# A hybrid sequence layer: convolution gates copied out by ScalarE, output projection summed in PSUM, second half of the merge and early P stages in written order

## The chip, the cores and the metric

One core of a Trainium2 chip runs the whole kernel. The metric is device time in microseconds, the median of the runs; a profiled execution is a run of its own. TensorE multiplies into PSUM (8 banks, each one output tile of 128x512 float32); VectorE and ScalarE read PSUM; GpSimd works on SBUF alone; transfers are queued on SyncE and ScalarE. Each engine takes its instructions strictly in its queue's order.

## The reference, cut to what matters

```python
h = rmsnorm(x, g_pre_mix)                     # x: 1024 tokens x 1024
proj = h @ w_in                               # u | conv x, B, C | q, k, v, forget | gates (3 x 1024)
ya = s5_mixer(u, ...)                         # 32 groups, 64 states each, scan over tokens
yb = B * conv3_causal(C * x_conv)             # 512 channels
yc = forgetting_attention(q, k, v, forget)    # 8 heads
merged = sum_b sigmoid(gate_b) * (y_b @ w_branch[b])
x = x + rmsnorm(merged @ w_out, g_post_mix)
x = x + rmsnorm(relu(rmsnorm(x, g_pre_mlp) @ w_ff1)**2 @ w_ff2, g_post_mlp)
```

All is float32. A product runs as three float32r products of high and low halves (high x high, high x low, low x high), so every weight tile is split: ScalarE writes the high half (H), VectorE or GpSimd subtracts to get the low half (L).

## The kernel before, in words

- **Head.** Tokens come in 8 tiles of 128 (t0 to t7). For each, ScalarE squares and sums (`x_square`), eight small operations make the inverse square root (`rsqrt1`, L79), and `x_norm` (L338) writes a diagonal matrix dg of it; `x_tr` (L361) multiplies a tile by its dg, which transposes and scales it at once. `x_split` makes hT, high and low.
- **Projections.** `proj_stream` (L263) hands out weight tiles of 128 columns, each times both halves of the tokens (th = 0, 1), 24 products per half, into two PSUM banks (tag `pj`). The consumer empties the bank: `conv_cons` (L798) for the convolution's x, c and b (four steps j), `gate_cons` for the 24 gates g. In between, generators for the S5 branch are run by a clock that the program keeps itself (`spawn`, `poll`): a generator yields the time after which it is to go on. For c and b VectorE multiplies from the bank: vp = p_cc x xs, later ac = p_cb x ac.
- **V.** At L888 the two weight blocks wv1 and wv0 are split, with 16 projection steps between them, and `v_group` multiplies them. Gates stay on ScalarE.
- **Attention**, then the **merge**: for each half th, pair dp of column tiles and branch b, `merge_item` (L1217) multiplies y_b by wb, gates it (gl, ma) and adds on GpSimd; the last branch splits the sum into m, high and low.
- **Output projection.** `rows_item` (L1258) multiplies m by w_out, four tiles of contraction (kc) and half the columns (e) at a time: for kc 0 ScalarE copies the bank to acc, for kc 1 VectorE adds the bank to acc. In the second half `wo_last` does kc 1 for both e (weights wol, and woeh/woel split ahead from woer).
- **mix(t)** (L1282), per token tile: square of acc, inverse square root on GpSimd (n_t), scale by it and gpost (VectorE), add x (xr; GpSimd for t0 to t3, VectorE for t4 to t7), a second square and root, hr = acc x root x gmlp, then eight transposes (pth) and the operands of the first feed-forward product: h2 for t0 to t3, and for t4 to t7 the combinations tb, tm and T1 to T4, high and low. These are a Strassen-like scheme with seven products: P1 needs only h2, P6 and the others need T of all four late tokens. The mixes of t0 to t3 run under the second half of the merge, those of t4 to t7 under wol and the P1/P2 stages (`Pair.run_a`, weights wa0 to wa7).
- **Order.** Outside of blocks under `manual_schedule`, a scheduler may move instructions within each engine's queue; inside, the order of the program holds. In the program before, only the head and V stand in such blocks.

```python
tt(vp[:, 2 + th * HALF:2 + (th + 1) * HALF], ps, cvt["xs"][:, sl], MUL)    # L811
if accumulate: tt(dst, ps, dst, ADD)                                        # rows_item
tt(acc, acc, xr_, ADD, dve if th else pool)                                 # mix
yield MY1 if th else 8.0
```

## Time and profile before

| | |
|---|---|
| median of three runs | 1694.05 us (1692.35, 1694.05, 1694.09) |
| profiled execution | 1695.55 us, its span 1693.8 |
| TensorE busy | 1622.6 us (96%), 7815 instructions |
| VectorE busy | 1032.2 us (61%), 1548 |
| ScalarE busy | 693.6 us (41%), 1042 |
| GpSimd busy | 501.9 us (30%), 603 |

The span is the time from the first to the last instruction in the trace. Busy shares are means over stages with different limits; which wait ends last in a stage is read from the trace of that stage. The granted clock is the share of full speed that TensorE was given: 1.00 is 2.4 GHz, 0.50 is 1.2 GHz, values between are means over a stretch.

### The profile page before, as it was taken

The page shows a single profiled execution, that of the slowest core. Times are in us where ns is not written, and L with a number is a line of the kernel's source. Part 1 is how long each engine was busy: PE and PEld are TensorE (multiplying, and loading weights), DVE is VectorE, ACT ScalarE, POOL GpSimd, SP SyncE. Part 2 cuts the span into 40 slices and gives each one's busy share as a digit, 9 for nine tenths or more (in the row PEclk, how much of TensorE's full clock was granted, in tenths as well). Part 3 has the DMA queues.
Part 4 walks back from the last instruction along what each step waited for, and adds up shares of the span by engine and source line. Part 5 has one row for each costly group of instructions (what it writes and reads, how often), then busy time and mean ns, then how long its engine had stood idle before and what let it go on. Part 6 is the DMA issues. An engine that isn't in the chain of part 4 may idle for free.

```text
span 1693.8 us, 21052 instructions
## 1 busy us (share of the span) xinstructions
PE 1622.6 (96%) x7815; PEld 1334.8 (79%) x7815; DVE 1032.2 (61%) x1548; ACT 693.6 (41%) x1042; POOL 501.9 (30%) x603
## 2 busy tenths in 40 slices
...
GB/s 162 122 42 77 83 68 103 108 99 7 216 174 142 213 47 218 117 168 58 255 262 97 193 205 91 138 163 189 183 181 143 166 344 373 254 199 195 178 100 50
DMA packets 186034, 261.73 MB, mean 155 GB/s; under 512 B 24752, under 2 KB 108764, under 8 KB 183884
## 3 DMA queue, kind: packets, MB, share of 16 engines
...
q8 instruction: 61, 1.00, 0.2%
q14 instruction: 41, 0.34, 0.1%
...
## 4 chain that ended last, share of the span: by engine, by line
PE 64%; DVE 9%; POOL 5%; DMA 5%; issue 4%; ACT 3%; SPq 1%; DVEq 0%; ACTq 0%; POOLq 0%
PE p_g L122 13%; PE P L122 11%; PE pb L122 3%; PE p_q L122 3%; PE pv L122 3%; PE P4f L122 3%; PE P7f L122 3%; PE P3f L122 3%; PE P6f L122 3%; PE P5f L122 3%; PE P2f L122 3%; PE P1f L122 2%; PE ps L122 2%; PE av L122 2%; PE pt L126 2%
## 5 line engine op out<-in xcount | busy, mean ns | idle before, releaser
L65 DVE TENSOR_TENSOR st<-x,st 128x1024 fp32r<-128x1024 f32 x70 | 86.7, 1250 | 77.4 <-ACT st L73 74.4
L122 PE MATMUL p_g<-hT,w_g_1H 128*128 128x512 f32 x384 | 126.4, 407 | 5.1 <-ACT g L831 3.5
L122 PE MATMUL p_g<-hT,w_g_0H 128*128 128x512 f32 x384 | 126.9, 406 | 2.8 <-DVE ac L65 2.8
L73 ACT ACTIVATE st<-x 128x1024 fp32r<-128x1024 f32 x70 | 73.6, 1059 | 98.5 <-PE P6f L122 16.6
L65 POOL TENSOR_TENSOR w2s<-w2s 128x512 f32<-128x512 f32 x32 | 44.0, 1375 | 232.1 <-DMA w2s<-in_w_ff 232.1
L65 POOL TENSOR_TENSOR s<-w1r 128x512 f32<-128x512 f32 x32 | 52.4, 1659 | 167.4 <-DMA w1r<-in_w_ff 156.4
L122 PE MATMUL pb<-yH,wb_0L 128*128 128x512 f32 x192 | 77.5, 403 | 11.8 <-DVE wb_0L L65 11.7
L65 DVE TENSOR_TENSOR sl<-x,sh 128x1024 fp32r<-128x1024 f32 x42 | 56.6, 1352 | 47.4 <-ACT sh L73 47.4
L122 PEld LDWEIGHTS p_g<-hT,w_g_1H 128*128 128x128 f32 x384 | 69.3, 192 | 17.5 <-ACT g L831 4.0
L122 PEld LDWEIGHTS p_g<-hT,w_g_0H 128*128 128x128 f32 x384 | 70.0, 191 | 14.8 <-DVE ac L65 3.2
L122 PE MATMUL pb<-yH,wb_0H 128*128 128x512 f32 x192 | 77.0, 401 | 2.1 <-DVE macc L68 2.1
L65 POOL TENSOR_TENSOR fa<-fa,gfin 128x512 f32<-128x512 f32 x16 | 25.5, 1606 | 178.0 <-ACT fjk L1654 178.0
L122 PE MATMUL p_g<-hT,w_g_1L 128*128 128x512 f32 x192 | 76.6, 399 | 0.0
L122 PE MATMUL pb<-yL,wb_0H 128*128 128x512 f32 x192 | 76.6, 399 | 0.0
L122 PE MATMUL p_g<-hT,w_g_0L 128*128 128x512 f32 x192 | 76.5, 398 | 0.0
L65 DVE TENSOR_TENSOR PT<-pt,PT 128x512 fp32r<-128x512 f32 (+2 forms) x96 | 53.0, 552 | 26.7 <-ACT PT L73 26.1
L73 ACT ACTIVATE PT<-pt 128x512 fp32r<-128x512 f32 (+2 forms) x96 | 47.0, 490 | 47.9 <-PE pt L126 43.5
L73 ACT ACTIVATE sh<-x 128x1024 fp32r<-128x1024 f32 x42 | 44.2, 1058 | 51.4 <-PE P3f L122 9.9
L1023 ACT ACTIVATE P<-ps,mx 128x128 f32<-128x128 f32 (+3 forms) x64 | 47.4, 740 | 32.0 <-DVE mx L1020 31.9
L65 POOL TENSOR_TENSOR macc<-macc,gl 128x512 f32<-128x512 f32 x16 | 27.8, 1748 | 101.6 <-DVE gl L68 101.6
L1020 DVE TENSOR_REDUCE mx<-ps 128x1 f32<-128x128 f32 (+3 forms) x64 | 48.1, 752 | 13.2 <-PE ps L122 13.1
L122 PEld LDWEIGHTS pb<-yH,wb_0L 128*128 128x128 f32 x192 | 37.0, 193 | 21.7 <-DVE wb_0L L65 13.9
(831 smaller groups left out, 4631.6 us busy)
## 6 DMA issues: line engine op xcount, KB each, us to landing
...
```

The costliest lines, as they stand in the source:

```text
L65: (eng or dve).tensor_tensor(o, x, y, op=op)
L73: act.activation(hi, src, AF.Copy, scale=scale)
L122: pe.matmul(o, l, r, start=start, stop=stop)
L126: pe.transpose(o, i, idn)
L1020: dve.tensor_reduce(mx, sv, axis=mybir.AxisListType.XY, op=MAX, negate=True)
L1023: act.activation(Pm[:, 0:kend].rearrange("p (c n) -> p c n", c=nch), sv, AF.Exp, bias=mx, accum_out=sm)
```

## The change

- Head: t1's root on GpSimd, the low half of w_u0 on VectorE; t4 to t7 are scaled in place (two on ScalarE, two on VectorE) and transposed with the identity.
- Convolution: ScalarE copies p_cc and p_cb to SBUF (vp, bs); VectorE multiplies 128x1024 from SBUF; xs has three buffers, vp and ac two.
- V: 12 projection steps ahead of the wv1 split, 20 (was 16) between the splits.
- Output projection: both halves of the contraction go to one bank, which stays open (`wps`); ScalarE copies it to acc after the second.
- From the output projection of the first half to the end of the early P stages VectorE, ScalarE, GpSimd and TensorE run in written order. The split of the last branch is spawned 2.0 later; mix has more yields; late mixes are spawned 4.0 apart (`MS`); P1 and P2 tiles are written one by one with the weight preparation of later pairs between them (`ff1_early`); one tile operation fewer makes tm. hr of all late tokens shares two buffers.

```diff
-    def x_norm(t0, n):
+    def x_rs(t0, n, eng=None):
...
+    def x_diag(t):
...
-        mm(o, xt[t][:, kt * P:(kt + 1) * P], dgs[t], True, True, 0.22)
+        if t < 4:
+            mm(o, xt[t][:, kt * P:(kt + 1) * P], dgs[t], True, True, 0.22)
+        else:
+            transp(o, xt[t][:, kt * P:(kt + 1) * P], ident)
...
-            x_norm(t, 1)
+            x_rs(t, 1, pool if t == 1 else None)
...
-                tt(vp[:, 2 + th * HALF:2 + (th + 1) * HALF], ps, cvt["xs"][:, sl], MUL)
+                act.activation(vp[:, 2 + th * HALF:2 + (th + 1) * HALF], ps, AF.Copy)
                 if th == 1:
-                    ac = cvt["ac"] = cv.tile([P, L], F, name=f"ac{j}", tag="ac")
+                    tt(vp[:, 2:], vp[:, 2:], cvt["xs"], MUL)
+                    ac = cvt["ac"] = cv.tile([P, L], F, name=f"ac{j}", tag="ac", bufs=2)
...
-                ac = cvt["ac"]
-                tt(ac[:, sl], ps, ac[:, sl], MUL)
+                act.activation(cvt["bs"][:, sl], ps, AF.Copy)
                 if th == 1:
+                    ac = cvt["ac"]
+                    tt(ac, ac, cvt["bs"], MUL)
...
+        for _ in range(12):
+            next(ps_)
         split(wv[1][1], wv[1][2], wv[1][0])
-        for _ in range(16):
+        for _ in range(20):
...
+    def merged(hi, lo, m):
+        split(hi, lo, m, scale=0.5)
+        yield 0.0
...
-                    split(mT[0, th, dt_ // 4][:, dt_ % 4, :], mT[1, th, dt_ // 4][:, dt_ % 4, :], macc[d], scale=0.5)
+                    spawn(merged(mT[0, th, dt_ // 4][:, dt_ % 4, :], mT[1, th, dt_ // 4][:, dt_ % 4, :], macc[d]), 2.0)
...
-                ps = mps(f"{name}p{t}")
+                if k0 == 0:
+                    wps[t, e] = mps(f"{name}p{t}")
+                ps = wps[t, e]
...
-                if accumulate:
-                    tt(dst, ps, dst, ADD)
-                else:
-                    act.activation(dst, ps, AF.Copy)
+                if k0:
+                    act.activation(accs[t][:, e * HALF:(e + 1) * HALF], ps, AF.Copy)
...
+        yield 1.5
         hr = hrow[0](f"hr{t}")
         rs = rms_scale(acc, hr, f"n1_{t}")
+        yield 5.0
         stt(acc, acc, rs, mixg[0], MUL, MUL)
         tt(acc, acc, xr_, ADD, dve if th else pool)
-        yield MY1 if th else 8.0
+        yield 2.5 if th else 5.0
         rs2 = rms_scale(acc, hr, f"n2_{t}")
         act.dma_start(x1_s[t], acc)
+        yield 5.0
         stt(hr, acc, rs2, mixg[1], MUL, MUL)
...
-        yield MY2 if th else 12.0
+        yield 5.0
...
-            tt(tm[:, 1], b12, tk["D"][:, :, cs], ADD)
...
-            stt(tm[:, 1], b22, -1.0, tm[:, 1], MUL, ADD)
+            tt(tm[:, 1], tk["D"][:, :, cs], tb[:, 0], SUB)
...
-                        spawn(mix(t))
+                        spawn(mix(t), MS * (t % 4))
...
+    def ff1_early(p, nxt):
+        p[0].run_p1()
+        nxt[0]()
+        yield
+        p[0].run_p2()
+        yield
+        p[1].run_p1()
+        nxt[1]()
+        yield
+        p[1].run_p2()
+        yield
...
+    ordered = tc.manual_schedule(engines={mybir.EngineType.DVE, mybir.EngineType.Activation, mybir.EngineType.Pool, mybir.EngineType.PE})
+    ordered.__enter__()
     new_acc(range(4), lt)
...
+    for i in range(0, KC, 2):
+        nxt = [p.prep_a for p in pairs[i + 2:i + 4]] if i + 2 < KC else [s_[0] for s_ in stages[:AH]]
+        for _ in ff1_early(pairs[i:i + 2], nxt):
+            poll()
+    settle()
+    ordered.__exit__(None, None, None)
```

How the queues move at three places. In the rows a number behind an underscore is the program's buffer number; of a name such as acc_8737 the number tells tokens apart.

VectorE's queue at the first convolution step, before (vp, ac and w_cc as above; CA belongs to the S5 branch):

```order
L65 TENSOR_TENSOR CA_1128<-CA_1128,Cx_1129 128x1152
L758 MEMSET S_1416 128x8
L65 TENSOR_TENSOR vp_1167<-p_cc_00_1107,xs_1076 128x512
L65 TENSOR_TENSOR vp_1167<-p_cc_01_1170,xs_1076 128x512
L60 TENSOR_SCALAR ac_1196<-vp_1167,cwcol 128x1024
L65 TENSOR_TENSOR w_cc_0L<-r_cc_1200,w_cc_0H 128x1024
L68 SCALAR_TENSOR_TENSOR ac_1196<-vp_1167,cwcol,ac_1196 128x1024 x2
L65 TENSOR_TENSOR ac_1196<-p_cb_00_1202,ac_1196 128x512
```

and now:

```order
L65 TENSOR_TENSOR CA_1124<-CA_1124,Cx_1125 128x1152
L771 MEMSET S_1415 128x8
L65 TENSOR_TENSOR w_cc_0L<-r_cc_1197,w_cc_0H 128x1024
L65 TENSOR_TENSOR vp_1163<-vp_1163,xs_1072 128x1024
L60 TENSOR_SCALAR ac_1193<-vp_1163,cwcol 128x1024
L68 SCALAR_TENSOR_TENSOR ac_1193<-vp_1163,cwcol,ac_1193 128x1024 x2
L65 TENSOR_TENSOR Kq_1253<-Kq_1253,dg 16x8x16
L65 TENSOR_TENSOR w_cb_0L<-r_cb_1336,w_cb_0H 128x1024
L65 TENSOR_TENSOR ac_1193<-ac_1193,bs_1228 128x1024
```

The products from PSUM are gone from the queue; two products of 128x1024 from SBUF have come, and the three operations of ac stand together.

ScalarE's queue at the start of V, before (g: gates; wvH: the high half of wv1, then of wv0; so: S5's output):

```order
L785 ACTIVATE so_3038<-pz_3029 128x1024
L73 ACTIVATE wvH_3078<-r_wv_2660 128x2112
L831 ACTIVATE g_3092<-p_g_00_3022,bgcol 128x512
L832 DMA gt_s_115<-g_3092 128x512
L831 ACTIVATE g_3120<-p_g_01_3095,bgcol 128x512
L832 DMA gt_s_115<-g_3120 128x512
L73 ACTIVATE w_g_0H<-r_g_3020 128x1024
L73 ACTIVATE wvH_3082<-r_wv_3080 128x2048
```

and now:

```order
L798 ACTIVATE so_3046<-pz_3037 128x1024
L848 ACTIVATE g_3098<-p_g_00_3030,bgcol 128x512
L849 DMA gt_s_115<-g_3098 128x512
L848 ACTIVATE g_3126<-p_g_01_3101,bgcol 128x512
L849 DMA gt_s_115<-g_3126 128x512
L73 ACTIVATE wvH_3086<-r_wv_2668 128x2112
L73 ACTIVATE w_g_0H<-r_g_3028 128x1024
```

Both halves of a gate tile now stand ahead of the first wvH.

VectorE's queue in the late mixes, before (acc_8741 to acc_8744 are tokens 4 to 7, hr_8916, hr_8968 and the two hr_9027 their rows):

```order
L68 SCALAR_TENSOR_TENSOR hr_8916<-acc_8741,n_4r,gmlp 128x1024
L65 TENSOR_TENSOR acc_8744<-wl_9042,acc_8744 128x512
L68 SCALAR_TENSOR_TENSOR acc_8743<-acc_8743,n_6r,gpost 128x1024
L65 TENSOR_TENSOR acc_8744<-wl_9056,acc_8744 128x512
L65 TENSOR_TENSOR acc_8743<-acc_8743,xr_9025 128x1024
L68 SCALAR_TENSOR_TENSOR hr_8968<-acc_8742,n_5r,gmlp 128x1024
L68 SCALAR_TENSOR_TENSOR acc_8744<-acc_8744,n_7r,gpost 128x1024
L65 TENSOR_TENSOR wa1L<-w1h_8945,wa1H 128x1024
L65 TENSOR_TENSOR acc_8744<-acc_8744,xr_9084 128x1024
L65 TENSOR_TENSOR o_0_9139<-P_0_9126,s_0_9111 128x512
L68 SCALAR_TENSOR_TENSOR hr_9027<-acc_8743,n_6r,gmlp 128x1024
L68 SCALAR_TENSOR_TENSOR hr_9027<-acc_8744,n_7r,gmlp 128x1024
```

and now, from the row of token 5 on (acc_8736 to acc_8738 are tokens 5 to 7):

```order
L68 SCALAR_TENSOR_TENSOR hr_9002<-acc_8736,n_5r,gmlp 128x1024
L65 TENSOR_TENSOR wa4L<-w1h_9192,wa4H 128x1024
L68 SCALAR_TENSOR_TENSOR acc_8737<-acc_8737,n_6r,gpost 128x1024
L65 TENSOR_TENSOR acc_8737<-acc_8737,xr_9075 128x1024
L65 TENSOR_TENSOR o_2_9216<-P_2_9203,s_2_9177 128x512
L65 TENSOR_TENSOR tb_9245<-pth_9234,b11f 128x512
L65 TENSOR_TENSOR tm_9244<-pth_9239,tb_9245 128x512
L65 TENSOR_TENSOR tb_9245<-pth_9239,tb_9245 128x512
L65 TENSOR_TENSOR tm_9244<-bdf,tb_9245 128x512
L65 TENSOR_TENSOR B_9092<-pth_9239,B_9091 128x4x128
L65 TENSOR_TENSOR T_9088<-tm_9244,T_9087 128x4x128
L65 TENSOR_TENSOR T_9090<-tb_9245,T_9089 128x4x128
```

The four rows hr stood close together, ahead of wa2L; now each token's work and the low half of a later weight alternate. hr of token 6 follows seven rows further on, behind the last two T, wa5L, o_3 and the scale and add of token 7.

## Rows read from the trace of the kernel before

**Rows 1.** The timeline of TensorE, two starts: the first product of each of two groups of four output tiles (48 products of 128x512 lie between them). Columns, in this and every timeline below: start in us, duration in us, engine, line, operation, output<-inputs, shape, count, and in brackets the engine's idle time before it and who ended it.

```profile
1004.73 0.39 PE L122 MATMUL wo100p<-wo_0H,m 128*128 128x512 f32 x1
...
1015.61 0.39 PE L122 MATMUL wo101p<-wo_0H,m 128*128 128x512 f32 x1
```

**Rows 2.** Busy time by stretches of 20 us: width, busy us (and instructions) of TensorE, its weight loads, VectorE, ScalarE and GpSimd, then the granted TensorE clock, DMA share and GB/s.

```profile
100.00:120.00 20.00, 17.39 (x70) 13.88 (x69) 11.25 (x12) 1.06 (x1) 19.53 (x32) 0.91 0.19 53
...
920.00:940.00 20.00, 17.87 (x76) 14.28 (x75) 11.51 (x11) 5.55 (x9) 11.45 (x25) 0.91 0.48 157
...
960.00:980.00 20.00, 11.29 (x52) 8.82 (x51) 14.30 (x13) 5.69 (x10) 12.41 (x18) 0.88 0.44 143
...
980.00:1000.00 20.00, 20.00 (x82) 16.29 (x82) 13.34 (x18) 7.34 (x11) 9.06 (x11) 0.86 0.78 270
...
1060.00:1080.00 20.00, 12.45 (x52) 9.94 (x53) 12.51 (x14) 7.89 (x14) 11.52 (x24) 0.73 0.34 96
...
1080.00:1100.00 20.00, 20.00 (x98) 16.69 (x98) 18.20 (x29) 15.09 (x25) 0.00 (x0) 1.00 0.54 161
```

**Rows 3.** The timeline of TensorE at its waits from the head to the start of the attention's V.

```profile
15.82 1.16 PE L122 MATMUL ptx<-dg,x 128*128 128x128 f32 x8 [0.81 <-ACT dg L345]
...
110.35 0.73 PE L122 MATMUL p_cb<-hT,w_cb_0H 128*128 128x512 f32 x2 [2.61 <-DVE vp L65]
...
149.88 0.73 PE L122 MATMUL p_cb<-hT,w_cb_0H 128*128 128x512 f32 x2 [1.09 <-DVE vp L65]
...
206.62 0.73 PE L122 MATMUL p_cx<-hT,w_cx_0H 128*128 128x512 f32 x2 [2.72 <-DVE ac L65]
...
250.27 0.72 PE L122 MATMUL p_g<-hT,w_g_0H 128*128 128x512 f32 x2 [2.80 <-DVE ac L65]
...
373.17 0.73 PE L122 MATMUL p_g<-hT,w_g_1H 128*128 128x512 f32 x2 [3.54 <-ACT g L831]
```

**Rows 4.** VectorE and ScalarE at the first convolution step.

```profile
109.62 0.67 DVE L65 TENSOR_TENSOR vp<-p_cc,xs 128x512 f32<-128x512 f32 x1
...
107.55 1.06 ACT L73 ACTIVATE w_cc_0H<-r_cc 128x1024 fp32r<-128x1024 f32 x1 [7.62 <-PE p_cc L122]
```

**Rows 5.** ScalarE at the start of V.

```profile
370.57 1.96 ACT L73 ACTIVATE wvH<-r_wv 128x2112 fp32r<-128x2112 f32 x1 [9.42 <-DMA ya_s<-so]
...
372.44 0.67 ACT L831 ACTIVATE g<-p_g,bgcol 128x512 f32<-128x512 f32 x1
```

**Rows 6.** TensorE at its waits in the second half of the merge.

```profile
926.70 0.50 PE L122 MATMUL pb<-yH,wb_0L 128*128 128x512 f32 x1 [2.13 <-DVE wb_0L L65]
...
958.51 0.50 PE L122 MATMUL pb<-yH,wb_0L 128*128 128x512 f32 x1 [0.85 <-DVE wb_0L L65]
...
965.76 0.50 PE L122 MATMUL pb<-yH,wb_0L 128*128 128x512 f32 x1 [1.48 <-DVE wb_0L L65]
...
979.62 0.80 PE L122 MATMUL pb<-yH,wb_0L 128*128 128x512 f32 x1 [7.23 <-DVE wb_0L L65]
```

**Rows 7.** VectorE, and in the last row GpSimd, in the second half of the merge.

```profile
955.40 3.05 DVE L65 TENSOR_TENSOR wb_0L<-r_wb,wb_0H 128x1024 fp32r<-128x1024 f32 x1
...
973.42 2.27 DVE L68 SCALAR_TENSOR_TENSOR acc<-acc,n_3r,gpost 128x1024 f32<-128x1024 f32 x1 [2.73 <-POOL n_3r L62]
...
976.21 3.35 DVE L65 TENSOR_TENSOR wb_0L<-r_wb,wb_0H 128x1024 fp32r<-128x1024 f32 x1
...
984.59 1.22 DVE L65 TENSOR_TENSOR wb_0L<-r_wb,wb_0H 128x1024 fp32r<-128x1024 f32 x1
...
975.77 2.72 POOL L65 TENSOR_TENSOR acc<-acc,xr 128x1024 f32<-128x1024 f32 x1 [1.16 <-DVE acc L68]
```

**Rows 8.** TensorE at its waits in the P stages.

```profile
1066.25 0.79 PE L122 MATMUL P<-h,wa1L 128*128 128x512 f32 x1 [11.95 <-DVE wa1L L65]
...
1070.68 1.11 PE L126 MATMUL pth<-ident,hr 128*128 128x128 f32 x8
...
1076.30 0.50 PE L122 MATMUL P<-h,wa2L 128*128 128x512 f32 x1 [1.30 <-DVE wa2L L65]
...
1111.70 0.50 PE L122 MATMUL P<-h,wa7L 128*128 128x512 f32 x1 [0.40 <-DVE wa7L L65]
```

**Rows 9.** VectorE in the late mixes and the P stages.

```profile
1050.19 1.28 DVE L68 SCALAR_TENSOR_TENSOR hr<-acc,n_4r,gmlp 128x1024 f32<-128x1024 f32 x1 [2.00 <-POOL n_4r L62]
...
1100.64 0.68 DVE L65 TENSOR_TENSOR o<-P,s 128x512 f32<-128x512 f32 x1
...
1102.37 0.68 DVE L65 TENSOR_TENSOR tb<-pth,b11f 128x512 f32<-128x512 f32 x1
```

**Rows 10.** ScalarE there.

```profile
1096.61 1.06 ACT L73 ACTIVATE wa6H<-w1h 128x1024 fp32r<-128x1024 f32 x1 [1.24 <-DMA w1h<-in_w_ff]
...
1100.57 0.58 ACT L1329 ACTIVATE tb<-pth 128x512 f32<-128x512 f32 x1
...
1101.36 0.63 ACT L1416 ACTIVATE o<-o 128x512 f32<-128x512 f32 x1 [0.21 <-DVE o L65]
...
1041.83 1.04 ACT L1176 ACTIVATE hr<-acc 128x1024 f32<-128x1024 f32 x1
```

**Rows 11.** GpSimd there: the first and the last of the eight small operations of one inverse square root.

```profile
1034.10 0.19 POOL L62 TENSOR_SCALAR n_4q<-n_4q 128x1 f32<-128x1 f32 x1 [22.29 <-ACT hr L1176]
...
1036.80 0.29 POOL L62 TENSOR_SCALAR n_4r<-n_4t,n_4r 128x1 f32<-128x1 f32 x1
```

More of the change, by code (lines that the diff above doesn't have):

```diff
@@ L336, in x_square @@
         act.activation(jk, xt[t], AF.Square, accum_out=xsq[:, t:t + 1])
-    def x_norm(t0, n):
+    def x_rs(t0, n, eng=None):
         sl = slice(t0, t0 + n)
-        rsqrt1(xrs[:, sl], xsq[:, sl], xtm[:, sl])
-        for t in range(t0, t0 + n):
-            dgs[t] = xp.tile([P, P], F, name=f"dg{t}", tag="dg", bufs=8)
-            if t == 3:
-                act.activation(dgs[t], ident, AF.Copy, scale=xrs[:, t:t + 1])
-            else:
-                ts(dgs[t], ident, xrs[:, t:t + 1], MUL)
+        rsqrt1(xrs[:, sl], xsq[:, sl], xtm[:, sl], eng)
+    def x_diag(t):
+        dgs[t] = xp.tile([P, P], F, name=f"dg{t}", tag="dg", bufs=4)
+        if t == 3:
+            act.activation(dgs[t], ident, AF.Copy, scale=xrs[:, t:t + 1])
+        else:
+            ts(dgs[t], ident, xrs[:, t:t + 1], MUL)
     pxs = {}
@@ L374, in hybrid_layer @@
             x_square(t)
-            if t == 3:
-                ut_tiles[0].split(pool)
-            x_norm(t, 1)
+            x_rs(t, 1, pool if t == 1 else None)
             if t == 0:
+                x_diag(0)
                 dve.tensor_copy(gcol, pgc[:, 0:KT])
+            elif t == 2:
+                x_diag(1)
+                x_diag(2)
+        ut_tiles[0].split()
+        x_diag(3)
         ut_tiles[1].split(pool)
@@ L389, in hybrid_layer @@
             x_square(t)
-        x_norm(4, 4)
+        x_rs(4, 4)
+        for t in range(4, NT):
+            if t % 2:
+                ts(xt[t], xt[t], xrs[:, t:t + 1], MUL)
+            else:
+                act.activation(xt[t], xt[t], AF.Copy, scale=xrs[:, t:t + 1])
     def x_rest():
@@ L803, in f @@
                 if th == 0:
-                    cvt["xs"] = cv.tile([P, L], F, name=f"xs{j}", tag="xs")
+                    cvt["xs"] = cv.tile([P, L], F, name=f"xs{j}", tag="xs", bufs=3)
                 act.activation(cvt["xs"][:, sl], ps, AF.Copy)
@@ L1353, in wo_item @@
         last = kc == 1 and e == 1
-        return rows_item(f"wo{th}{kc}{e}", wo_k, 4 * kc, e, range(4 * th, 4 * th + 4), lhs, kc == 1,
+        return rows_item(f"wo{th}{kc}{e}", wo_k, 4 * kc, e, range(4 * th, 4 * th + 4), lhs,
                          (lambda t: spawn(mix(t), 10.0 * (t % 4))) if last else None)
@@ L1370, in run @@
                         xh, xl = lhs(t, k)
-                        mm(ps, xh, wh, k == 0, False, 0.214)
+                        mm(ps, xh, wh, False, False, 0.214)
                         mm(ps, xh, wl, False, False, 0.214)
                         mm(ps, xl, wh, False, k == 3, 0.214)
-                    dst = accs[t][:, e * HALF:(e + 1) * HALF]
-                    tt(dst, ps, dst, ADD)
+                    act.activation(accs[t][:, e * HALF:(e + 1) * HALF], ps, AF.Copy)
                     if e:
-                        spawn(mix(t))
+                        spawn(mix(t), MS * (t % 4))
                     if (t, e) == WP:
-                        stages[0][0]()
+                        pairs[0].prep_a()
                     yield
@@ L1478, in run_a, with run_p1, run_p2 @@
             yield
+        def run_p1(self):
+            i = self.i
+            if i % 2 == 0:
+                s1t[i // 2] = lt.tile([P, 2, HALF], F, name=f"s1_{i}", tag=f"acc{(i // 2) % 4}")
+            self.s1 = s1t[i // 2][:, i % 2]
+            self.p1 = prod(f"P1_{i}", self.wa, 0, h2[0, 0], h2[1, 0])
+            act.activation(self.s1, self.p1, AF.Copy)
+        def run_p2(self):
+            i = self.i
+            p2 = prod(f"P2_{i}", self.wa, 4, h2[0, 1], h2[1, 1])
+            o = lt.tile([P, HALF], F, name=f"o11_{i}", tag="row", bufs=3)
+            tt(o, p2, self.s1, ADD)
+            put_a(i, "P1", o)
+            self.a11 = None
         def run_b1(self):
@@ L1522, in run_b3, with ff1_stages @@
             yield
-    def ff1_stages():
-        ps_ = [Pair(i) for i in range(NF)]
+    def ff1_early(p, nxt):
[9 more added lines that the diff above has]
+        yield
+    def ff1_stages(ps_):
         A = lambda p: [(p.prep_a, p.run_a)]
@@ L1528, in ff1_stages @@
         st = []
-        for p in ps_[:KC]:
-            st += A(p)
         for p in ps_[:KC]:
@@ L1740, in hybrid_layer @@
     r2 = r2_es.enter_context(pool_("r2"))
-    hlate = []
-    def hr_tile(name):
-        t = int(name[2:])
-        if t < 6:
-            return r2.tile([P, D], F, name=name, tag="hr", bufs=2)
-        if not hlate:
-            hlate.append(ws.tile([P, 2, D], F, name="hr67", tag="raw", bufs=2))
-        return hlate[0][:, t - 6, :]
-    hrow[0] = hr_tile
-    stages = ff1_stages()
+    hrow[0] = lambda name: r2.tile([P, D], F, name=name, tag="hr", bufs=2)
+    pairs = [Pair(i) for i in range(NF)]
+    stages = ff1_stages(pairs)
     run_items(wo1[:1], wo1[1:])
```

23 lines of the change are left out of this document (11 added, 12 removed).

## The prediction, as put on record before the changed kernel ran

> **What bounds the kernel now.** I read the busy shares first, then the busy time by stretches with TensorE's granted clock, then TensorE's waits one by one, and at each wait the queue of the engine named. TensorE is busy 96% of the span, so only its waits, and the stretches at half clock behind them, can be won. At full clock 48 products of 128x512 take 1015.61 - 1004.73 = 10.88 us, 2.72 for an output tile of 12 [rows 1], and eight transposes 1.04 [rows 8]. In 1080:1100 the clock is 1.00. In 100:120, which has one wait of 2.61, it is 0.91 on average: part of the stretch ran at 1.2 GHz instead of 2.4, and 0.09 x 20 = 1.8 us went with it [rows 2, 3]. I charge these 1.8 to each wait over 2 us and nothing to shorter ones.
>
> The losses that the change aims at:
> - **Convolution:** waits of 2.61, 1.09, 2.72 and 2.80, all on VectorE's vp or ac [rows 3]: 9.2, with three half-clock stretches of 1.8 14.6.
> - **Start of V:** 3.54 on a ScalarE gate [rows 3], with 1.8 behind it 5.3.
> - **Merge, second half:** 2.13, 0.85, 1.48 and 7.23, all on VectorE's wb_0L [rows 6]: 11.7; the clock of 920:940 (0.91) adds 1.8, that of 980:1000 (0.86 of a stretch without a wait) 2.8 [rows 2]: 16.3.
> - **Late mixes and P stages:** wol starts at 1015.61 + 10.9 = 1026.5. From there eight wol tiles, sixteen P tiles and four sets of transposes are 24 x 2.72 + 4 x 1.04 = 69.5 us of work, to 1096.0. The trace resumes after its last wait here at 1111.70 [rows 8] with 20 products of the last pair open and 8 of P6_0 and its followers issued early: 12 net, 2.7 us, so 1114.4. Lost: 18.4, of which 11.95 in one wait for wa1L.
>
> Together 54.6 us.
>
> **Part by part.** *Head.* Token 1's inverse square root goes to GpSimd: eight small operations in 3.0 us [rows 11], beside VectorE's for token 2 instead of ahead of it, so dg3, which ends the 0.81 wait [rows 3], is free earlier. The diagonals of tokens 1 and 2 come later, and their products fill that gap. Between nothing and 0.8 I take 0.3. Tokens 4 to 7 are scaled whole, two on ScalarE and two on VectorE (two instructions of about 1.06 each [rows 10]); their transposes replace as many products: nothing, hidden behind ut projections; 1 us if that cover is short.
>
> *Convolution.* TensorE waits because a PSUM bank of the projection is emptied by VectorE, which stands in its queue behind S5 work (vp starts at 109.62, right behind a CA). In the new order ScalarE copies these banks; it is busy 1.06 us of 100:120 [rows 2, 4], so a copy (about 0.6, like o and tb [rows 10]) starts when the tile ends. VectorE exchanges four PSUM operations of 0.67 a step [rows 4] for two of 128x1024 (1.22 [rows 7]), no more work. All four waits go. Late next is the S5 state for py: its VectorE chain was covered by projection tiles together with the waits that vanish. I keep back 0.6 for it: **14.0** (11 to 14.6).
>
> Here a rule speaks against the edit. Row first: the same 128x1024 subtraction takes 1.22 us at 984.59, and 3.05 and 3.35 at 955.40 and 976.21; the last runs beside a GpSimd addition (975.77, 2.72) [rows 7]. GpSimd is busy 19.53 of 100:120 [rows 2]. The Trainium skill, page "GPSIMD Engine Reference", section "Key points", says that GpSimd shares its SBUF interfaces with VectorE and contends with VectorE instructions that have two SBUF inputs. The new products vp x xs and ac x bs are of that kind, while the old ones took one input from PSUM; the trace agrees with the rule in the three rows named. By 1.22 each they cost nothing that TensorE sees; by 3.05 to 3.35 the eight of them add some 15 to 17 us to VectorE's queue, a part of which the S5 chain hands on. I stay near the first, since nothing but S5 waits for them, and the second sets the lower end of 11.
>
> *Start of V.* Twelve steps of the gate projection now stand before the wv1 split. In the old queue the split (370.57, 1.96 us) waits for the ya_s transfer, and gate g starts at 372.44 behind it [rows 5]; in the new one two gates pass first. The wait of 3.54 and its 1.8 go; the wv split in front of the following gate may cost 0.5. **4.8** (3.5 to 5.3). The 48 products that move ahead of the attention are the same work; later gate numbers shift through the attention, +-1.5, which I count as nothing.
>
> *Output projection in PSUM.* Sixteen VectorE additions of about 0.68 [rows 9] become ScalarE copies of 0.6. TensorE never waited for them; their worth is room on VectorE in the next part. All eight banks are held to the second half; those copies follow at once.
>
> *Merge in written order.* VectorE's queue no longer puts a token's scale, which waits for GpSimd (2.73 idle before 973.42), ahead of the next weight's low half at 976.21 [rows 7]. I followed the written queues pair by pair. With E the end of the output projection, six tiles are 16.3 and the transposes of token 0 end at E+17.4. ScalarE then copies h2 twice and b11f (0.6 each), the last behind a VectorE subtraction of 0.68, and splits wb111 (1.06): E+20.5; VectorE's low half 1.22: E+21.7. TensorE has two tiles first and wants it with the third product of pb121, at 17.4 + 5.4 + 0.5 = E+23.3. The slack of 1.6 is the smallest that I found. A contended low half (3.05 for 1.22) eats it, so I leave 2.5 us of waits over: **13.8** (8 to 16.3).
>
> *wol.* woeh and woel now stand ahead of wol on both queues and wait for the woer transfer: 0.5 lost (0 to 1.5).
>
> *Late mixes.* The queues are written, so a token's row hr can only come after all that stands before it. I walk them from the start of wol, A, with 1.28 for a scale, 1.22 for an add or low half, 0.68 for a PSUM tile on VectorE, 1.06 for a high half, 1.1 for a square, 0.6 for a tile on ScalarE, 3.0 for an inverse square root [rows 7, 9, 10, 11].
> - hr5: ScalarE's square of token 4 stands behind a copy of acc5 and wa0H (A+10.9), its second square behind a copy of acc6 (A+18.0); hr4 is at 22.3. wa1H follows the last wol copy, wa2H the copy of P1_0 (26.2); wa2L 27.4, token 5's scale and add 29.9, o11_0 30.6, on ScalarE its two operations and tb4 32.4, VectorE's four tile operations 35.1, T4 and the second square of token 5 36.8, s1 and wa3H 38.5, wa3L, o11_1, hr5: 41.7. TensorE wants hr5 at 21.8 + 6 x 2.72 + 1.04 = 39.2: a wait of 2.5.
> - hr6: from hr5 on s1_2 (whose buffer was acc5's), wa4H, wa4L, scale and add of token 6, o11_2, its two ScalarE operations, a square of token 7, tb5, four tile operations, T4, the square of token 6, s1, wa5H, wa5L, o11_3, scale and add of token 7, hr6: 20.7 us in one chain. TensorE has 1.04 + 4 x 2.72 = 11.9: a wait of 8.8.
> - hr7: the same way 12.8 us against 1.04 + 3 x 2.72 = 9.2: a wait of 3.6. The half-clock stretch behind it costs 1.8; those behind the first two vanish in the next wait.
>
> New losses 2.5 + 8.8 + 3.6 + 1.8 + 0.5 = 17.2 against 18.4: **1.2** (-6 to 18). One tile operation a token less is in the walk. The wait for wa1L goes; what is late next is hr6.
>
> **Sum:** 0.3 + 14.0 + 4.8 + 13.8 + 1.2 = 34.1. The profiled execution took 1695.55, so 1661.4; it lies 1.5 above the median of the runs shown (1694.05): **1660**.
>
> **Rivals.**
> 1. *The P stages flow.* If the row chains overlap better than my walk (a ScalarE queue that is free when I hold it blocked), all of the 18.4 goes: 51.3 saved, median 1642.8. For it: the old stage from 1080 on runs without a wait at VectorE 18.20 of 20 [rows 2], so the throughput is there. Against: the new order spreads the same latency chains over the tiles that want their ends. 0.2.
> 2. *Contention.* Low halves at 3.05 where GpSimd works: merge 8, convolution 11, V 4, late stage 0 with 0.3: 23.3 saved, 1670.7; with the late stage 5 worse 1676. This is the mechanism of the rule above. For it: 19.53 of 20 in 100:120 and the two slow rows. 0.2.
> 3. *Slower: the written ScalarE queue stalls the merge.* A token's second square waits for GpSimd's addition, and the next pair's high half stands behind it. If a token's GpSimd work (two inverse square roots of 3.0, one addition of 2.72 and four of the merge) passes the 17.4 us of a pair, the lag grows and each of four pairs waits like the 7.23 with its 2.8: 40 instead of 16.3; rows 3 us later each add some 10 to the late stage. Net 23.7 + 10 - 19.1 = 14.6 lost: 1708.6. Against it: GpSimd is busy 9 to 12.4 of 20 there [rows 2], about 10 of 17.4. 0.04.
> 4. *It does not do what it says:* ScalarE, kept in order, reaches the copies late, and the convolution waits stay half: 7 lost from the sum, 1667; that lies inside the range. 0.06.
>
> **How the numbers follow.** The forecast (late stage about level, 1653 to 1668) has 0.5. Slower by over 0.2% (3.4 us, about what a measurement of this kernel can tell from no change) needs rival 3, 0.04; within 0.2% would need rival 2 with a late stage worse by 20, 0.03 of its 0.2; faster is 0.93. The range of 8 in 10 takes in the forecast, rivals 1 and 4 and most of rival 2: 1640 to 1675.
>
> **What would show it.** After the change no p_cb, p_cx or first p_g product waits on VectorE, and 100:120 has a clock near 1.00; the gate wait at 373 is gone; pb waits in the second half sum to under 4; pth of tokens 5, 6 and 7 wait for hr, token 6 longest, near 9. Wrong would be: pth of token 6 without a wait (rival 1), wb low halves of 3 us with pb waits of 1 to 2 each (rival 2), pb waiting on ScalarE's wb_0H (rival 3).

## The result, and the profile after

The changed kernel took **1677.76 us** (median of four runs, 1674.73 to 1678.66), the kernel before beside it 1693.2: ratio 0.9908 [0.9891, 0.9926]. That is faster, as forecast, but by about half of the 34.1 us of the sum, and outside the range of 1640 to 1675. The profiled execution took 1678.06 (span 1676.3 against 1693.8).

The stretches below run from one first product on TensorE to another (the timeline's start times), so their gains add up (they are taken from unrounded times); the late term of the sum, 1.2, is split here into 1.7 and the 0.5 for wol. 48 gate products (10.9 us [rows 1]) moved from the attention into V; the table counts them where they were.

| stretch on TensorE | before | after | forecast gain | gain |
|---|---|---|---|---|
| head: start to first p_cx | 82.1 | 78.5 | 0.3 | 3.7 |
| convolution: p_cx to p_g | 168.1 | 159.2 | 14.0 | 8.9 |
| V: p_g to p_q | 198.0 | 191.4 | 4.8 | 6.6 |
| attention: p_q to first pb | 351.9 | 353.7 | 0 | -1.8 |
| merge, first half, and wo0: pb to last wo0 | 118.5 | 116.9 | 0 | 1.7 |
| **merge, second half:** last wo0 to wo100p | 86.1 | 81.7 | 13.8 | 4.3 |
| wo1 and wol: wo100p to first P | 43.5 | 43.5 | -0.5 | 0.0 |
| **late mixes, P stages:** P to first P1f | 331.1 | 337.1 | 1.7 | -6.1 |
| last stage: P1f to last P4f | 306.0 | 305.9 | 0 | 0.1 |
| sum | | | 34.1 | 17.5 |

One boundary hides something: the half-clock stretch behind the old wait of 2.80 on the first p_g lies behind that product, in the row of V (granted clock 0.83 in 250:260 before, so 1.7 us; 1.00 there now). The convolution's forecast had counted it.

TensorE's timeline after, at the waits that answer to [rows 3, 6, 8]:

```profile
158.45 3.16 PE L122 MATMUL pz<-gq,BD 128*128 128x128 f32 x16 [2.77 <-DVE gq L68]
...
366.92 0.39 PE L122 MATMUL pv<-wvH,hT 128*128 128x264 f32 x1 [0.33 <-ACT g L848]
...
663.78 0.69 PE L126 MATMUL pt<-ident,P 128*128 128x128 f32 x4 [2.56 <-DVE PT L65]
...
923.54 0.50 PE L122 MATMUL pb<-yH,wb_0H 128*128 128x512 f32 x1 [1.29 <-ACT wb_0H L73]
...
938.32 0.50 PE L122 MATMUL pb<-yH,wb_0L 128*128 128x512 f32 x1 [1.46 <-DVE wb_0L L65]
...
944.48 0.50 PE L122 MATMUL pb<-yH,wb_0H 128*128 128x512 f32 x1 [0.87 <-ACT wb_0H L73]
...
970.54 1.13 PE L126 MATMUL pth<-ident,hr 128*128 128x128 f32 x8 [2.48 <-DVE hr L68]
...
1046.59 1.97 PE L126 MATMUL pth<-ident,hr 128*128 128x128 f32 x8 [4.39 <-DVE hr L68]
...
1069.54 1.97 PE L126 MATMUL pth<-ident,hr 128*128 128x128 f32 x8 [9.32 <-DVE hr L68]
...
1083.81 1.73 PE L126 MATMUL pth<-ident,hr 128*128 128x128 f32 x8 [2.96 <-DVE hr L68]
```

The four waits of [rows 3] on vp and ac are gone, and the gate wait of 3.54 has become 0.33 (a second one of 0.78 is there before and after). In their place stands one wait for gq, the S5 stage's own chain. In the attention, where no wait was over 1.83 before, TensorE now waits 2.56 for VectorE ahead of a set of transposes; the clock is 0.91 in 660:680, where it was 1.00. In the merge the low halves still wait, and the high half wb_0H, ScalarE's, waits as well. Late, hr5, hr6 and hr7 wait 4.39, 9.32 and 2.96, where 2.5, 8.8 and 3.6 had been worked out.

The same stretches of 20 us as in [rows 2] or their successors, in the same columns:

```profile
100.00:120.00 20.00, 20.00 (x99) 16.31 (x98) 11.72 (x10) 4.71 (x6) 19.45 (x26) 1.00 0.25 63
...
140.00:160.00 20.00, 17.23 (x96) 14.82 (x95) 17.53 (x21) 6.94 (x8) 14.15 (x15) 0.98 0.18 50
160.00:180.00 20.00, 20.00 (x92) 16.89 (x92) 7.54 (x7) 4.80 (x6) 14.13 (x37) 0.94 0.41 109
...
920.00:940.00 20.00, 16.73 (x75) 12.99 (x75) 16.18 (x17) 7.77 (x13) 15.84 (x21) 1.00 0.52 178
940.00:960.00 20.00, 16.72 (x74) 12.62 (x73) 15.27 (x18) 9.01 (x15) 15.74 (x22) 1.00 0.66 212
...
1060.00:1080.00 20.00, 10.68 (x42) 8.82 (x42) 14.78 (x19) 12.59 (x22) 10.45 (x19) 0.74 0.38 131
```

100:120 is full, with a clock of 1.00 and ScalarE at 4.71 instead of 1.06. Behind the wait for gq the clock is 0.98 and 0.94 in two stretches, so some 0.4 and 1.2 us went there. In the merge GpSimd, the fifth engine column, is busy 15.84 and 15.74 of 20; it was 11.45 and 12.41 in [rows 2], and the forecast had reckoned with about 10 of 17.4. Over the whole second half of the merge about the same GpSimd operations took 58.2 us, where they had taken 47.7. In 1060:1080 the clock is 0.74.

Now one pair of the merge, engine by engine. GpSimd: the first and last operation of token 1's inverse square root with the slowest between them, then the additions.

```profile
909.91 0.19 POOL L62 TENSOR_SCALAR n_1q<-n_1q 128x1 f32<-128x1 f32 x1
...
911.32 2.31 POOL L62 TENSOR_SCALAR n_1t<-n_1r,n_1q 128x1 f32<-128x1 f32 x1
...
914.56 0.29 POOL L62 TENSOR_SCALAR n_1r<-n_1t,n_1r 128x1 f32<-128x1 f32 x1
...
914.88 3.52 POOL L65 TENSOR_TENSOR ma<-ma,gl 128x512 f32<-128x512 f32 x2
918.36 2.40 POOL L65 TENSOR_TENSOR acc<-acc,xr 128x1024 f32<-128x1024 f32 x1
```

ScalarE and VectorE in the same pair:

```profile
918.43 0.63 ACT L73 ACTIVATE m<-ma 128x512 fp32r<-128x512 f32 x1 [9.88 <-POOL ma L65]
918.97 1.07 ACT L73 ACTIVATE h<-pth 128x512 fp32r<-128x512 f32 x2
921.95 0.60 ACT L1345 ACTIVATE b11f<-pth 128x512 f32<-128x512 f32 x1 [1.92 <-DVE h L65]
922.44 1.05 ACT L73 ACTIVATE wb_0H<-r_wb 128x1024 fp32r<-128x1024 f32 x1
```

```profile
914.88 2.36 DVE L68 SCALAR_TENSOR_TENSOR acc<-acc,n_1r,gpost 128x1024 f32<-128x1024 f32 x1 [0.79 <-POOL n_1r L62]
...
919.09 2.22 DVE L68 SCALAR_TENSOR_TENSOR m<-ma,m 128x512 fp32r<-128x512 f32 x1 [1.25 <-ACT m L73]
...
921.23 1.28 DVE L65 TENSOR_TENSOR h<-pth,h 128x512 fp32r<-128x512 f32 x2
...
923.52 1.22 DVE L65 TENSOR_TENSOR wb_0L<-r_wb,wb_0H 128x1024 fp32r<-128x1024 f32 x1 [0.25 <-ACT wb_0H L73]
```

The last wo0 ends at E = 899.6. The forecast had ScalarE copy h2 at E+17.4 and split wb_0H until E+20.5. It copies at E+19.4, because the split of m in front of it waits for GpSimd's ma, and ma stands behind a root that takes 4.94 us (909.91 to 914.85) instead of the 3.0 of [rows 11]. VectorE's acc waits for that root too, then runs 2.36 beside GpSimd's ma, and m 2.22 beside acc+xr; so h comes at 921.23, b11f behind it, and wb_0H ends at 923.49, E+23.9. The slack was 1.6, the delay 3.4, and TensorE waits 1.29 and 0.53.

### The profile page after: what moved, and what is told of

Same layout as the page of the kernel before. It is cut to its first block, busy times and chain, and to the rows that moved or that the text cites. A ratio compares the mean times of both kernels' runs of the same rounds, so it can differ in the third digit from the quotient of the medians.

```text
span 1676.3 us, 20921 instructions
## 1 busy us (share of the span) xinstructions
PE 1614.5 (96%) x7783; PEld 1330.6 (79%) x7783; DVE 1028.2 (61%) x1511; ACT 702.7 (42%) x1060; POOL 517.9 (31%) x610
## 4 chain that ended last, share of the span: by engine, by line
PE 44%; DVE 6%; POOL 3%; issue 3%; ACT 3%; DMA 1%; SPq 0%; ACTq 0%; DVEq 0%; POOLq 0%
PE P L122 11%; PE pb L122 5%; PE P4f L122 3%; PE P7f L122 3%; PE P3f L122 3%; PE P6f L122 3%; PE P5f L122 3%; PE P2f L122 3%; PE P1f L122 2%; PE p_g L122 2%; PE wo101p L122 1%; PE wo100p L122 1%; PE wo001p L122 1%; PE wo000p L122 1%; PE p_q L122 1%
## 5 line engine op out<-in xcount | busy, mean ns | idle before, releaser
L848 ACT ACTIVATE g<-p_g,bgcol 128x512 f32<-128x512 f32 x48 | 32.8, 683 | 53.4 <-PE p_g L122 53.2
```

Source lines behind the costliest of these rows:

```text
L848: act.activation(g, ps, AF.Tanh, bias=bgcol[:, i:i + 1], scale=0.5)
```

## The experiments

Two theories stood for most of the missing 17 us. **Roots:** the inverse square roots on GpSimd (eight small dependent operations) are the late link in the merge and in the late mixes. **Place:** the written order puts work in the wrong place of a queue. Beside both, contention of VectorE and GpSimd. Below, "merge" is the stretch from the last wo0 to wo100p and "late" the one from the first P to the first P1f; a ratio is to the kernel before, run beside the kernel named, with its 95% interval. Stage times repeat where the code is the same: the merge stretch took 80.1 to 81.7 in five profiles (197.8 to 199.0 from first pb to wo100p), the late stretch 337.1 to 337.3 in seven, the convolution 158.5 to 161.3 in ten.

### Convolution

**e10, convolution as before** (copies and their buffer counts undone, the rest as changed):

```diff
-act.activation(vp[...], ps, AF.Copy); tt(vp[:, 2:], vp[:, 2:], cvt["xs"], MUL)
+tt(vp[:, 2 + th * HALF:...], ps, cvt["xs"][:, sl], MUL)
...
-act.activation(cvt["bs"][:, sl], ps, AF.Copy); tt(ac, ac, cvt["bs"], MUL)
+tt(ac[:, sl], ps, ac[:, sl], MUL)
```

> The changed kernel, with the convolution's copies put back: VectorE takes vp and the last product out of PSUM itself, ScalarE only xs. The stretch from the first p_cx to the first p_g is 159.1 us in the changed kernel, 168.2 in the kernel before. Theory A (ScalarE's copies are what shortened it, by 9, less than the forecast 14.0 because GpSimd's table chain then ends last): 167 to 169 here, the whole 8 to 10 slower than the changed kernel. Rival B (the head's earlier end, or another order, shortened it): at most 3 back.

Measured: 1691.11, ratio to before 0.9990 [0.9980, 1.0001]; the stretch took 168.7. Two of its four old waits on TensorE, back in place:

```profile
203.20 1.04 PE L122 MATMUL p_cx<-hT,w_cx_0H 128*128 128x512 f32 x2 [2.73 <-DVE ac L65]
...
246.85 0.72 PE L122 MATMUL p_g<-hT,w_g_0H 128*128 128x512 f32 x2 [2.80 <-DVE ac L65]
```

Theory A in the stage. The whole lost 13.4, more than the stage's 9.5. Another 1.8 lies in the row of V, half clock behind the wait on p_g (0.91 in 240:260, 1.00 in the changed kernel); the other 2 are not explained (its profiled span was 10.0 above the changed kernel's).

**e4, last table level left out:**

```diff
+if e == 6 and j:
+    pool.memset(TR[:, :, k:2 * k], 1.0); pool.memset(TI[:, :, k:2 * k], 0.0); continue
```

> The changed kernel, leaving out the last doubling of the S5 tables TR and TI on GpSimd for all state groups but the first (two constant fills instead), a probe of GpSimd's load in the convolution. In the changed kernel the convolution (first p_cx to first p_g) took 159.1 us with one wait of 2.77 for VectorE's gq at 158.45, beside VectorE's CA at 4.28 and scalar products at 4.18 a pair. Theory A (GpSimd's table chain, which did not come earlier with TensorE, and its contention with VectorE set that wait): it goes, and the stretch takes 154 to 156. Rival B (gq is late by its place in VectorE's queue behind the new products of vp and ac): VectorE still reaches it late, the wait stays over 2 and the stretch within 1 of 159.

This kernel leaves out a part of S5's tables, so it is a probe and no version to use. Measured: 1673.4 in a single run; the stretch took 154.7 and the wait for gq was gone. VectorE ahead of gq, in the changed kernel and then in this one, and this one's 140:160:

```profile
145.95 4.18 DVE L68 SCALAR_TENSOR_TENSOR ac<-vp,cwcol,ac 128x1024 f32<-128x1024 f32 x2
150.06 4.28 DVE L65 TENSOR_TENSOR CA<-C1t,prr 128x128 f32<-128x128 f32 x7
...
157.62 1.28 DVE L68 SCALAR_TENSOR_TENSOR gq<-G,py 128x512 f32<-128x512 f32 x2 [0.90 <-ACT G L786]
```

```profile
144.64 2.60 DVE L68 SCALAR_TENSOR_TENSOR ac<-vp,cwcol,ac 128x1024 f32<-128x1024 f32 x2
147.16 1.50 DVE L65 TENSOR_TENSOR CA<-C1t,prr 128x128 f32<-128x128 f32 x7
...
151.72 1.28 DVE L68 SCALAR_TENSOR_TENSOR gq<-G,py 128x512 f32<-128x512 f32 x2 [0.90 <-ACT G L790]
```

```profile
140.00:160.00 20.00, 20.00 (x114) 17.45 (x113) 16.02 (x23) 7.56 (x9) 7.25 (x11) 1.00 0.25 76
```

The same instructions, two scalar products for ac and seven for CA, take 4.18 and 4.28 with GpSimd's table work beside them and 2.60 and 1.50 without: 4.36 us. This agrees with the rule cited in the prediction (Trainium skill, "GPSIMD Engine Reference", section "Key points"), for instructions with two SBUF inputs. Theory A. That the stretch is shorter by about the same, 4.5 us, is partly chance: VectorE was late by these 4.36, and what TensorE lost by it is the wait of 2.77 and the 1.6 at half clock behind it.

### Merge

**e7, no written order in the merge** (`ordered` entered only ahead of wo1):

```diff
-ordered.__enter__()          # ahead of new_acc(range(4), lt)
+ordered.__enter__()          # ahead of run_items(wo1[:1], wo1[1:])
```

> The changed kernel, with the merge's second half (and the output projection of tokens 0 to 3) left to the scheduler, as before; the written order begins only at the second output projection. Theory A (the written order is worth what was claimed for it, and GpSimd's lateness took part of it back): without it the merge stretch is about that of before, 84 to 87 us against 81.7, the whole 2 to 5 slower than the changed kernel. Rival B (the written order gains nothing there, and what was won came from the projection in PSUM and the later split of m): the stretch stays within 1.5 of 81.7 or shrinks.

Measured: 1683.04, 0.9936 [0.9911, 0.9960]; merge 83.5, and from first pb to wo100p 203.3 against 198.6 and, before, 204.6. So the written order was worth some 4.7 us over the two stretches that it covers; the merge alone lost 1.8, between what A and B said and little more than the 1.6 by which the same code varies there.

**e2, split of m later; e3, acc+xr on VectorE:**

```diff
-    spawn(merged(..., macc[d]), 2.0)
+    spawn(merged(..., macc[d]), 8.0)       # e2
...
-tt(acc, acc, xr_, ADD, dve if th else pool)
+tt(acc, acc, xr_, ADD, dve)                # e3
```

> The changed kernel, with the merge's hook for the second half's weight product placed six units of the written order later (8.0 for 2.0), so that ScalarE's split of m stands later in its queue. In the changed kernel output-projection end to the next output projection's start is 81.7 us (86.0 before, 72 forecast), with waits of 1.29, 0.87 and 0.66 for ScalarE's wb_0H. Theory A (the split stands in ScalarE's queue ahead of wb_0H and waits for a late ma, so its place is the cause): the three waits for wb_0H go, the stretch shrinks by 3 to 6. Rival B (GpSimd is late by its amount of work, and VectorE by contention with it, wherever the split stands): the waits move to another name, and the stretch stays within 1 of 81.7.

> The changed kernel, with the addition of the residual to acc of tokens 0 to 3 done by VectorE instead of GpSimd (four GpSimd operations of 2.4 to 3.4 us less, four of VectorE more at 1.2 each). Theory A (GpSimd's work and its contention with VectorE make the merge's rows late): VectorE's operations of 2.2 to 2.4 beside it shrink to about 1.2, and the merge stretch (81.7) loses 3 to 6. Rival B (the place of ScalarE's m split in its queue is the cause): at most 1 us is won in that stretch, and VectorE's four more additions may cost as much.

Measured: e2 1678.40, 0.9909 [0.9888, 0.9931], merge 78.6; e3 1678.68, 0.9908 [0.9886, 0.9930], merge 80.8. In e2 the waits of 1.29 and 0.87 for wb_0H went, and others came:

```profile
941.34 0.79 PE L122 MATMUL pb<-yH,wb_0L 128*128 128x512 f32 x1 [2.18 <-DVE wb_0L L65]
...
963.02 0.50 PE L122 MATMUL pb<-yH,wb_0H 128*128 128x512 f32 x1 [3.13 <-ACT wb_0H L73]
```

Both are half an answer. In e2 the stretch shrank by 3.1, while the stretch ahead of it grew by 2.2: from first pb to wo100p it took 197.6, next to the 197.8 to 199.0 of the unchanged code, so nothing is gained. (Ahead of it TensorE waits 2.12 where the changed kernel waits 2.05, but here the clock fell behind it, to 0.91 in 800:820, and there it stayed at 1.00.) In e3 GpSimd's load fell to 12.19 and 13.16 of 20 and the stretch did not follow. VectorE took the four additions over, at 2.20 for the one of token 1, so this shows only that less work for GpSimd at that price gains nothing.

**e5, roots on VectorE** (all tokens of the mixes):

```diff
-rsqrt1(rs, sq, tm, pool)
+rsqrt1(rs, sq, tm, dve)
```

> The changed kernel, with the two inverse square roots of every token in the mixes done by VectorE instead of GpSimd: eight small operations take 2.0 us there (5.52 to 7.53 in the head), on GpSimd 3.0 alone and 4.94 in the merge (909.91 to 914.85). Theory A (the latency of these roots on GpSimd, beside its contention, is what VectorE's written queue waits on, with the next pair's weight behind it): the merge stretch (81.7 us) loses 4 to 7, the waits of 4.39, 9.32 and 2.96 for hr5, hr6 and hr7 lose some 2 each by the two roots per token, the whole is 7 to 12 faster than the changed kernel. Rival B (VectorE itself carries the bound; it gets 16 us more work over the two stages): the waits only change their names, both stretches stay within 2.

Measured: 1679.56, 0.9913 [0.9886, 0.9941]: no gain in all, but two opposite ones inside. Merge 76.9, 4.9 less: A. Late 342.5, 5.4 more: outside of what either theory said. The first and last operation of token 1's root on VectorE, 2.01 us in all where GpSimd took 4.94:

```profile
909.33 0.15 DVE L62 TENSOR_SCALAR n_1q<-n_1q 128x1 f32<-128x1 f32 x1
...
911.12 0.22 DVE L62 TENSOR_SCALAR n_1r<-n_1t,n_1r 128x1 f32<-128x1 f32 x1
```

And TensorE's late waits with VectorE's longest new one:

```profile
1043.85 1.97 PE L126 MATMUL pth<-ident,hr 128*128 128x128 f32 x8 [6.45 <-DVE hr L68]
...
1068.32 1.97 PE L126 MATMUL pth<-ident,hr 128*128 128x128 f32 x8 [10.21 <-DVE hr L68]
...
1084.29 1.97 PE L126 MATMUL pth<-ident,hr 128*128 128x128 f32 x8 [4.70 <-DVE hr L68]
```

```profile
DVE n_7q L62 <- ACT hr L1195: 2.9, 1, 2.9
```

In the written queue a root takes its 2.0 us ahead of everything behind it, and once it waits 2.9 for ScalarE's square there. From the first P to the third of these waits VectorE is busy 49.8 us, 9.0 more than in the changed kernel, and the stretch is 5.3 longer. That is B's mechanism, with a size that B did not expect. On GpSimd, a root held up only what needs its result.

### Late mixes, and both together

**e1, late order as before:**

```diff
-ordered.__exit__(...)   # after the early P stages
+ordered.__exit__(...)   # after the merge's settle; P stages, yields and hr6, hr7 as before
```

> The changed kernel, with the late mixes and P stages put back to the order before (the written order ends after the merge's settle; hr6 and hr7 again in two buffers of their own; head, convolution, V, output projection and merge as changed). In the changed kernel the stretch from the first P tile to the end is 643.1 us, in the kernel before 637.1. Theory A (the written late order costs these 6.0, mostly in the waits of 4.39, 9.32 and 2.96 for hr5, hr6 and hr7): these three waits go, the old one for wa1L comes back, the stretch takes 636 to 639, the whole about 1672 and 5 to 6 us less than the changed kernel. Rival B (the late loss comes from what the earlier stages hand on, such as VectorE and GpSimd being behind when wol starts): the stretch stays within 2 of 643 and so does the whole.

Measured: 1673.26, 0.9881 [0.9861, 0.9901]; late 333.5 against 337.1, and 4.5 less in all, though the two intervals overlap. A in the waits, which are gone; in size a little less (639.6 from the first P to the end, 3.6 won). TensorE's wait for wa1L came back, shorter than the 11.95 of [rows 8], another came for wa7L, and VectorE's waits for GpSimd (name, engine and tile waited for, us, times, longest) show what remains:

```profile
1039.14 0.79 PE L122 MATMUL P<-h,wa1L 128*128 128x512 f32 x1 [7.44 <-DVE wa1L L65]
...
1088.38 0.79 PE L122 MATMUL P<-h,wa7L 128*128 128x512 f32 x1 [6.42 <-DVE wa7L L65]
```

```profile
DVE acc L68 <- POOL n_5r L62: 5.3, 1, 5.3
DVE acc L68 <- POOL n_6r L62: 2.9, 1, 2.9
DVE hr L68 <- POOL n_7r L62: 2.9, 1, 2.9
DVE acc L68 <- POOL n_7r L62: 2.6, 1, 2.6
```

With three more of 2.1 to 2.6 that is 21.0 us of VectorE waiting for roots, in 80.

**e6, both edits** (e5 and e1):

> The two edits together: inverse square roots of the mixes on VectorE, and late mixes and P stages in the order before. If both theories hold (roots on GpSimd in the merge; written late order), the merge stretch loses 4 to 7 and the stretch from the first P tile to the end some 4 as in the run with that order alone: about 1665 to 1668. If the roots are not the cause it is the time of that run alone, 1673. If VectorE is the bound of the late stage, its 8 more us there lengthen the waits of 7.44 for wa1L and 6.42 for wa7L: 1670 or more.

Measured: **1656.76**, 0.9775 [0.9748, 0.9803]; merge 76.9, late 317.6. VectorE's longest wait in the same 80 us and TensorE's one long wait:

```profile
DVE o L65 <- issue: 3.0, 1, 3.0
```

```profile
1051.28 1.06 PE L126 MATMUL pth<-ident,hr 128*128 128x128 f32 x8 [2.71 <-DVE hr L68]
```

No wait for a root is left. The expectation had 1665 to 1668: with the scheduler free to put other work between the small operations the roots pay 15.9 us in the late stretch, not nothing.

**e9, the kernel before with roots on VectorE** (the one line of e5):

> The kernel before, with nothing changed but the inverse square roots of the mixes on VectorE instead of GpSimd. Theory A (the roots' latency on GpSimd, 3.0 to 4.9 us each, is what both the merge's second half and the late mixes wait for, whatever the order of the rest): the merge stretch (86.0 us from the last wo0 product to the first of the next projection) goes to 78 to 82, the stretch from the first P tile to the first P1f (331.3) to about 318 as in the run with both edits, the whole 15 to 20 faster than the kernel before: 1674 to 1679. Rival B (the roots only pay together with the change's new order and its room on VectorE): under 6 faster, 1688 or more.

Measured: 1675.04, 0.9897 [0.9884, 0.9911]; merge 76.9 (from 86.1), late 321.2 (from 331.1). A: one word of the old kernel is worth as much as the whole change. The trace of before had shown this link already: VectorE waited 18.7 us for roots in the second half of the merge and 17.7 in 1044:1124. The longest of each:

```profile
DVE hr L68 <- POOL n_0r L62: 5.6, 1, 5.6
```

```profile
DVE acc L68 <- POOL n_5r L62: 3.7, 1, 3.7
```

The two edits look independent (0.9897 x 0.9881 of e1 = 0.9779, and both together gave 0.9775), but stage by stage they are not. In the merge the change alone won 4.3 (6.0 in e1's profile), the roots alone 9.1 and both 9.2: they mostly remove the same time. In the late stretch the change with e1's order lost 2.5, the roots alone won 9.9 and both 13.5. The product comes out right because these two departures nearly cancel.

**e11, e6 with the split later; e12, e6 with no written order at all:**

> Roots on VectorE and late order as before (1656.8), and the split of m six units later in the merge. Theory A (ScalarE's place of that split still costs: waits of 1.19 and 0.79 for wb_0H are left in the merge): the merge stretch goes from 76.8 to 74 or 75, the whole 1654. Rival B (with short roots ma is early and the split's place costs nothing; the rest is VectorE's throughput at 18 to 19 of 20): within 1 of 76.8, no gain.

> Roots on VectorE and late order as before, with no written order anywhere after the attention: merge, projections and mixes are all left to the scheduler. Theory A (the written order keeps a gain of its own, 4.6 us over merge and projection by the run without it): 1660 to 1662. Rival B (the written order only worked round the late roots, so that without them there is nothing left for it): within 2 of 1656.8, the merge stretch within 1.5 of 76.8.

Measured: e11 1654.76, 0.9775 [0.9761, 0.9790], merge 73.0; e12 1657.30, 0.9793 [0.9774, 0.9812], merge 76.9, late 318.3. In e11 the stage did as A says, and the whole cannot be told from e6. In e12 B holds: without late roots the written order of e6 has nothing left to win. With the later split (e11) the merge stretch is shorter still; that split was not tried without the written order. e6 and e11 are the best versions here, some 21 to 23 us below the changed kernel.

### Head

**e8, diagonals for tokens 4 to 7 again** (and no scaling in place)**:**

```diff
-if t < 4: mm(o, xt[t][...], dgs[t], ...)
-else: transp(o, xt[t][...], ident)
+mm(o, xt[t][...], dgs[t], ...)
```

> The changed kernel, with tokens 4 to 7 of the head transposed by products with their diagonals again, as before. Theory A (each product with a diagonal costs TensorE twice a transpose: it shows as two records, 64 for 32 tiles at 0.116 us): the head's last ptx ends 3 to 4 later, the whole is some 3.7 slower than the changed kernel. Rival B (my prediction: hidden behind the u projections): within 1.

TensorE's groups in 18:50, in the kernel before and in the changed one (operation, tiles, shape, count, busy us, mean ns, idle):

```profile
L122 PE MATMUL ptx<-dg,x 128*128 128x128 f32 x84 | 10.6, 278 | 0.1
```

```profile
L126 PE MATMUL ptx<-ident,x 128*128 128x128 f32 x32 | 4.4, 276 | 0.0
L122 PE MATMUL ptx<-dg,x 128*128 128x128 f32 x21 | 3.2, 284 | 0.1
```

Measured: e8 has the first row again (84 products, 10.6 us) and its first p_cx at 81.4. Three kernels with diagonals have it at 81.4 to 82.1, eleven without at 75.2 to 79.3. So A in the stage; the whole, 1679.26, 0.9910 [0.9887, 0.9934], cannot show 3 us.

## Why the prediction was right and wrong

- **What failed most: the merge's second half, 13.8 forecast and 4.3 measured.** The step was "I followed the written queues pair by pair", with a smallest slack of 1.6. The walk had the order right and two links missing: the split of m in ScalarE's queue ahead of h2, and the root in GpSimd's queue ahead of ma and of VectorE's acc. It also took GpSimd's load from the old, slower stage ("about 10 of 17.4"; it was 15.8 of 20), and roots at 3.0 from [rows 11], where VectorE stood idle, when beside VectorE's work one took 4.94. Waits on pb sum to 6.6, where the prediction's sign was under 4, and a pth wait of 2.48 comes on top. e5 (4.9 us from the roots) and e11 (another 3.9 from the split's place) bring the stretch to 73.0: 13.1 of the 13.8 were there to be had, with two more edits.
- **Late mixes: 1.7 forecast without wol, -6.1 measured.** The walk of the queues held (16.7 us of waits against 14.9). Mis-sized was the clock: "those behind the first two vanish in the next wait", 1.8 in all. 69.7 us passed from first P to first P6_0 (1094.5); 16 tiles and four sets of transposes are 47.7, the waits 16.7, so 5.3 went at half clock, seen in the 0.74 of 1060:1080 and in transposes of 1.97 where [rows 8] has 1.11. Each of the three waits brought such a stretch (0.91 in 1040:1060 and 0.91 in 1080:1100 as well). Against the 66.2 of before this is a loss of 3.5. The other 2.5 come behind P6_0, where the same 1152 products up to P1f take 267.4 for 264.9 at a clock of 1.00: counted from start to start, what passes the even pace of 0.23 us a product sums to 6.0 against 3.5, all of it at small waits of up to 1.05, mostly on low halves.
- **Convolution: mechanism right, size off, 14.0 forecast and 10.6 measured** (8.9 in its row and 1.7 in the row of V). e10 shows that the copies did it. The term that failed is "I keep back 0.6" for the S5 chain: it cost 4.4, a wait of 2.77 and the half clock behind it, and e4 shows contention as the cause. The bounds were there, 11 to 14.6 with "3.05 to 3.35" for contended products, and the choice of the near end was wrong; even the far end was a little too high.
- **Head: 0.3 forecast, 3.7 measured.** "Their transposes replace as many products: nothing" was wrong: 32 transposes take 4.4 us and the products for the same tiles came as 64 records.
- **V: 4.8 forecast, 6.6 in its row,** of which 1.7 belongs to the convolution: 4.9, as forecast. Its row is the same within 0.1 in all twelve profiles with this code but e10's.
- **Attention: 0 forecast, -1.8 measured.** "later gate numbers shift through the attention, +-1.5, which I count as nothing" left out a wait: the set of transposes at 663.78 waits for VectorE, 2.5 to 3.0 us in each of the twelve kernels with the moved gate products, and neither the kernel before nor e9 has a wait over 1.84 there. The row is 1.0 to 4.5 longer than before in these twelve, never shorter. That the moved products cause the wait was not tested by itself.
- **Rivals.** Contention (1670.7, or 1676 with a late stage worse by 5) came nearest, partly by luck: contention was the cause in the convolution; in the merge it only lengthened roots and rows, while the low half behind the wait of 1.29 ran at 1.22. Flowing P stages did not come with this change, but e6 found 13.5 of its 18.4 us. The stalled ScalarE queue showed its sign, waits on wb_0H, at 1.29 at most and not growing. That the change would not do what it says is out: no p_cb, p_cx or first p_g product waits.

What stays open: 2 us of e10, what causes the wait in the attention, and how much of the first pair's remaining 1.19 in e5 is contention.
